# Three pairs instead of two in the token-ordered end of a seven-product down projection, four more weight buffers for it, and a new written order of all 4836 steps

## The chip, the cores and the metric

The kernel runs on one core of one Trainium2 chip. The metric is the device time of one execution in microseconds. Before the change three executions took 626.68, 627.62 and 628.64 us; the median is 627.62.

## The reference

One layer of a hybrid decoder for 512 tokens of width 1024, all in float32: a conditioned RMS norm, one input projection that feeds a gated linear recurrence (512 channels) and an eight-head sparse attention, an output projection, a residual, a second conditioned norm, and a squared-ReLU MLP with 4096 hidden features. What matters here is its end:

```python
h = modulate(rms_norm(x, pre_norm_mlp[l]), sh2, sc2)
y = jnp.square(jax.nn.relu(h @ w_ff1[l])) @ w_ff2[l]
x = x + (1.0 + g2[:, None, :]) * rms_norm(y, post_norm_mlp[l])
```

## The kernel before

**Precision.** A float32 factor is split into a high part `hi`, rounded to the format that TensorE takes at full rate, and a rest `lo` (`split_f32`: a copy on ScalarE or VectorE, then a subtraction). A product is three matmuls (`mm3`): hi by hi, hi by lo, lo by hi, each of 512 output columns here. All matmuls are recorded at line 396, transposes at 400, ScalarE work at 407, VectorE and GpSimd work at 441, loads and the stores of the output at 483.

**Down projection.** The hidden features are 32 tiles `fT[0..31]` of 128 features by 512 tokens, taken in 16 pairs (`NP`). The tokens are cut into two halves, the 1024 output columns into two halves and each pair is its own inner cut of two, so that each pair is a two-by-two block product done with seven products instead of eight. Products "6", "7" and "1" need sums of weight blocks and of token halves and are done in a first pass (`first_pass`, weights `A0` to `A15`, interleaved with the up projection). Products "2" to "5" are done in a second pass (`second_pass`, weights `B0` to `B15`). A PSUM bank tag stands for each: "2" is `f`, "3" is `s`, "4" is `pv`, "5" is `tp`, with two banks each, one for each of two 128-token blocks `t` (0 and 1) of a token half.

For each pair of the second pass two raw weight tiles, 512 KB each, are loaded; two subtractions form block differences in them; each is split into hi and lo (128 x 1024); and the two `fT` tiles of the pair are split into four `fs` tiles (`operands`). Product "2" needs the first half of the lower weight tile, "3" its second half, "4" and "5" the halves of the upper one. A pair is 4 products x 2 blocks x 3 matmuls = 24 matmuls.

**The last phase.** For the first `NP - G_LAST` = 14 pairs the loop goes pair, product, block. For the last two (`G_LAST = 2`) it goes block first: all of block 0 (4 products x 2 pairs x 3 = 24 matmuls), then all of block 1. When a product of a block is complete, VectorE and others combine it with the running sums `acc`, and `finish` computes the norm of the finished 128 output rows, scales, adds the residual and stores. `finish(t + 2, ...)` comes after product "4" of block t and `finish(t, ...)` after product "5". So while TensorE works at block 1, the other engines finish the rows of block 0. In `finish` a sum of squares runs on ScalarE (with `accum_out`), a product with `g2row` on VectorE or GpSimd (tile names `fT<-ar,g2row`), the small `stat` steps turn the sum into a scale, and a `scalar_tensor_tensor` with the residual `r` comes ahead of each store.

**Buffers.** `Weights` holds a ring of 4 raw tiles and of 4 hi/lo pairs for all weights from start to end (`RAW_BUFS`, `PART_BUFS`), `f_tile` a ring of 8 `fs` tiles, two pairs' worth. The pool `fp` holds `h2` and `h2l`, the operands of the up projection, and `g2row`.

**What sets the order.** The program is first recorded as 4836 steps, numbered in the order in which a greedy planner puts them down, and then issued in the order of the text `PLAN`: two characters are one step (90 letters, so `C^` is step 12 x 90 + 84 = 1164). Each engine's queue is that text with only the engine's own steps left in. `PLACE` gives for each step with a choice the engine: a is ScalarE, d is VectorE, p is GpSimd. Nothing is reordered at run time: an instruction that waits holds what is behind it on its engine. The steps' numbers are the same in both kernels up to the end of the up projection (step 4086), so the two texts can be compared there step by step.

**Before the MLP.** The gate branch of the recurrence (`g0` to `g3` of `proj`) leaves TensorE through one of two `f` banks; ScalarE copies each to SBUF (`act(rnn["g"][:, n, :512], ps, AF.Copy)`, recorded as `r<-f`), and the next projection in that bank waits for the copy.

Of the kernel before, what the change touches and what calls it, by code (L numbers as in the profile page):

```python
# [33 lines left out]
G_LAST = 2  # L34
# [56 lines left out]
    '000O0P020Q0106400R0S0T0U0V0M074p4q084r0a0W0y040b4sGX4t090c030&0d0X0A554u0C4v054w0e4x0(0-4y0Y0H0N4z4!0D4:'  # L91
    '4;0I0B4<0)0Z0f0E0.0,4D0J0z0/0_0=0^0K0!0{0L0|0*0g0>0h4=0?0F4>0i1O0}0j0:4?104@0~0G0]12144[0k1P0;0l0m0#110@'
    '131j1C0n0%1E0o1F0p151k1G1v171619180+1H0q1A1D540r1B1l561J1=0s1M0t1I0u1N0v1K0w1Q0x1>1U1m0$1R1T1n0[1S1W0<1L'
    '1o1V1X1w1p1q1r1]1a1s1b2M1h1x1d1t1^1@1$1Z1[201f1?1u1c1i1Y572L2X2Q2R1y1_1e1+1&2Y2S1{1g1|1!1)2N1#211}2T1-1;'
    '232&2s27221*2O1:2U1%2P1z2(292V2Z1(2x1/2v1.2t24262y2z302C1,1~2w1<2A2)2u2D2W3125282}2!322F2#2I2B2H2$2|2J2a'
    '2d372E2K2~2G3S2c2j2g2e2f382b2l2i333V3T2k39352r2h2n342/2m2q363W2*2p3X2%2o2-3*3!3U2,3x3#2<2]3c3Y2?2=3y3C3Z'
    '3I3$2:3a2{2@583d2^3O3F3D3z3b3%3e3h3&3J3n3+3P3(3L3i3o3,3R3)3t4#3k3/4H3?3u4%3:3q4F3{3@45463w3A473G3M484M2.'
    '3|3f4O494C3l3r4A3<4N4B3-4g3=4G4$4h4i4k4l4m4j4Q4^4&4n4P4+4o4,4-4]GY4(4.2+2>4~4S5L504)2;514*3]5K4/2[4_3~4{'
    '4d2_3^5Y3E413K3Q52425D3B5X5M4|4}59533H3j445E5h5A5B5C435F5H5G3N5g5J3p3v5O3g3m5I5N5S3;5$3[5P3s4b7%5T3.5R3>'
    '4a3_3}4J5Q5#5Z5U5V5a5b5i5j5k4I5-5W5l5m5d5n5o5p5q5,5r4X5s7&4V5t5u4K5e627)6;4c6-5v4L5w6<6.6/5x6=5y615z5f6d'  # L100
    '5!5%6>6e4W6f7>6N674U6_6M5c6:7(68696@6A7?6V6B6{6?6C4e4R6D5_6E5&4Z4T6g6F4Y6G6H6I6U5(5)6[6J6|7+6K4f6q6}6L7|'
    '6h6O5*6p6P6i5+6]6^816Q6~6R6j6y5.5/6S6x6T6W5:726k5{716l6X6m6n5;5<7a6Y5=5>6a5?7b5@5[6Z5]73706o7c5^5}5|6r5~'
    '6c607C636s7B646t7R6u656v6w6b667N746z6!7S7D6#6$6%8L7z757T6&7@7!766(7[7o7]7}6)7~80777*7#788279836*847A7s85'
    '7t7p6+7q86877M88897r8A8B7w7u8V8W7vGW8Z8C8D8X7x7E8b7^8K8d937F8Y947,8E7-977_7.GZ957G997H7y7I9&7/8e4E7J8j9('
    '7K8k9)7L9+7O8h8F9,7P8f6,8G8O8i9E8P8QGa987Q7U9A9F7V8R9I7W9K7X9J9G7Y8M8S7Z8g7$7d8T7:7e8c9:7fG@9H8^8_9L8{9;'
    '7g8a9<7h7i968U8|8l8}7j8~9MAO8mG]90919*929B7;8u8q8v7kAP9=AU8w9N8x7l8y8r8z8!8#9l8$G^8%8&8(8)8*8n8+G_7m9C8o'
    '8,8t8-G[9m8.9T7<8p9D8N9V7=8s8/9O8:8H8;8<8=AV8>8I9W9n8?9r9o9s9X8@9Y9Z9aAS8[9b9R9c9p9d9t9e9v9f9w9x9q9y9g9U'
    'A59z8J9h9!AQAW9#ARA67{9$9iA79%AE9SAvB.A88]7nApAF9-AGAHAq9u9.AXA9B/AwAI9/9>AT9?9@Ar9[At9]9j9^9PAAAJAgCbAB'
    'CcAY9_C9AxAK9{AD9|9}9~AZ9QCdAdAcCiA.CAA/AuA0AhAzA!CNCjCkHPA>CpCqAsA#AfA?CrA:AeA@AiC#A<A$C$A%ALC%AaAjAbAM'
    'C+A&C,COA1C-A=BDBEANC/AyBHB5C:BJC;A[BFC<A(A;AkBtBIA]A2BGACA)BKHQBLA*AlA3B6BuB1BMA+B2BRB3C=A^BPC_A_BNC>A,'  # L110
    'A|BvAmA-A~B,BwB79kBhAoC1B-HRA}B4C3C2B8HSCWBnB9BiB0CHC4HeAnA4A{CBCVCQBAHbBjBBBoCIBpB:BCBcBqBkCXCJCRBlCUBd'
    'BmCLCKBrBxCSB#CMC{BsB$ByBzCaC@B%C[C|DVC]C~B!D0CTB(D1D2DWCZD3D4D6CeD7B)ChD8CYD9DACoDBCuDCDDCmDEB*DFCsDGCf'
    'DHDICwB+DJCzDKC)DLDMClC!C^DOCvDPB;DND$CtCnD%DQDRFhD+D@C*D[DSD]CxDTDUC&DuDYDeDvDZCyDaDbDcC?BSDdDhD^D_DiDw'
    'C(DjB&DkD)BODlDyDmD!DnDzD&DoDfBeB<D{BQD|ECD,D}DpBTC}D(DqDrD*DsDxD~E6B=EDBUE0D5D#E1DtBYEsFjBZEtB?BaEuD-E2'
    'CgEvEwD.BbBfB@E7BVB[E3C.BWB]B^D=B|ExD?E*B_E+E8BXE,EAE9GUFlE4EEEaEbD/E[BgEgE]HEEhEBC5GVB}E^D;B~E_L(D<EFE{'
    'EiDXE|D>FAF%EcL&EeFBFCFnFIB{EdFJEfE-C0FKFdEjHFFeFfE5FgE=E>C6F|C7EkE?EQHJD:EGE.ElCPFkEHEmE/EWE;EIEJErC8FR'
    'FSEoEKFTEXCCFLEqELB>FoFMEYEREpCDFNEMFPENCEEOF}ESEPEZF~F&F4F5HNF,ETF-G0H>G,FiG-EUH?HKFmEyEVF6F<F=F.G3CGE}'
    'E~EzF>E!EnF0G4F1HLE#CFE$E%F2F_F7H@GxF:F8FpG.F3E&GrFUE(FqF9FrFtG6GsFuFsGvGyG/FzGtFvE)FwG:F{G1H4F!F#F$FxH5'
    'GzG;FDF(G8FyF)G2FGG9GAE@F*HGG5GBH6H[F+E:H]HAF;H^HBFHGCFOH_H8G7F@E<GDHCH{H|GEF[HpHqHOFQGNGOHHHDGPGQHrF]H7'
# [417 lines left out]
class Weights:  # L537


    def __init__(self, clk, pool, raws):  # L540
        self.clk, self.pool, self.raws, self.jobs, self.index = clk, pool, raws, [], {}
        self.queue, self.loaded, self.parts, self.raw_live, self.part_live = [], {}, {}, [], []
        self.l = self.s = 0
        self.slots, self.taken = [], {}
# [1265 lines left out]
```

## Time and profile before

| what | us |
|---|---|
| median of three executions (lowest, highest) | 627.62 (626.68, 628.64) |
| the profiled execution | 627.82 |
| its span, first to last instruction | 626.0 |
| outside the span | 1.8 |
| TensorE / VectorE / ScalarE / GpSimd busy | 596.3 / 539.2 / 346.1 / 209.1 |
| from the end of the last matmul to the end of the span | 12.0 |

The profiled execution is 0.20 us above the median. A matmul's record covers 0.39 us for 512 columns, but successive ones start 0.227 us apart, so the busy sum of TensorE says little and its waits are read from the starts. VectorE's records overlap a little as well: three successive 128 x 512 steps of 0.68 us start 0.60 us apart.

### The profile page before, as it was taken

The numbers are of one execution on the slowest core, as the hardware profiler recorded it, in microseconds if no ns is written. First come the engines' busy times: TensorE is split into PE (matmuls) and PEld (weight loads), VectorE is DVE, ScalarE is ACT, GpSimd is POOL, SyncE is SP. The second block draws the span as 40 slices with busy tenths as digits, with TensorE's granted clock in tenths as the row PEclk, the third lists the DMA queues.
The fourth block names the chain that finished last, engine by engine and source line by source line (L and its number), as shares of the span: only waits on it lengthen the run. The fifth ranks groups of instructions, "written<-read, shape, count | busy, mean of one in ns | idle before, by whom it ended". The sixth has DMA issues, their size and how long they took to land.

```text
span 626.0 us, 9043 instructions
## 1 busy us (share of the span) xinstructions
PE 596.3 (95%) x3060; PEld 497.9 (80%) x3060; DVE 539.2 (86%) x1072; ACT 346.1 (55%) x696; POOL 209.1 (33%) x209
## 2 busy tenths in 40 slices
PE   7999999998999999989999999999999999999992
PEld 6888788966777898869887888888887888878881
DVE  5986988979999988988888968787688789999897
ACT  6654525698999999687251220322322247465563
POOL 5001301652663175453204547641351231000113
PEclk9999999999999999999999999999999999999997
DMA  8968895430503302015664334254544426756613
GB/s 351 416 250 318 320 299 191 131 136 1 202 2 129 141 2 102 1 35 176 229 222 168 115 133 137 101 169 157 180 135 147 155 69 204 238 179 202 198 56 134
DMA packets 29430, 102.15 MB, mean 163 GB/s; under 512 B 3268, under 2 KB 3524, under 8 KB 29384
## 3 DMA queue, kind: packets, MB, share of 16 engines
q1 hardware_dynamic: 29240, 101.50, 46.4%
q8 instruction: 24, 0.39, 0.3%
q14 instruction: 22, 0.18, 0.1%
q10 hardware_dynamic: 144, 0.07, 0.0%
HBM read 99.47 MB, written 2.10 MB: 162 GB/s over the span
## 4 chain that ended last, share of the span: by engine, by line
PE 73%; DVE 11%; DMA 6%; ACT 5%; issue 3%; DVEq 0%; SPq 0%; ACTq 0%
PE f L396 36%; PE s L396 14%; PE pv L396 13%; PE tp L396 7%; DMA ar<-in_ada_t 4%; PE tp L400 4%; DVE r L441 3%; ACT p L407 2%; DVE fT L441 2%; ACT r L407 2%; DVE ar L441 1%; DMA raw_A11l<-in_wd 1%; DMA raw_A10l<-in_wd 1%; DVE p L441 1%; DMA r<-in_x 1%
## 5 line engine op out<-in xcount | busy, mean ns | idle before, releaser
L396 PE MATMUL f<-h,hi_f 128*128 128x512 f32 x224 | 87.7, 392 | 0.0
L396 PE MATMUL f<-h,lo_f 128*128 128x512 f32 x224 | 87.2, 389 | 0.0
L396 PE MATMUL f<-h2l,hi_f 128*128 128x512 f32 x224 | 87.2, 389 | 0.0
L407 ACT ACTIVATE fT<-f 128x512 f32<-128x512 f32 x30 | 17.8, 594 | 71.2 <-PE f L396 71.2
L396 PEld LDWEIGHTS f<-h,hi_f 128*128 128x128 f32 x224 | 42.1, 188 | 8.8 <-issue 0.2
L396 PEld LDWEIGHTS f<-h2l,hi_f 128*128 128x128 f32 x224 | 42.0, 188 | 8.6
L396 PEld LDWEIGHTS f<-h,lo_f 128*128 128x128 f32 x224 | 42.0, 188 | 8.5
L396 PE MATMUL f<-hi_o,h 128*128 128x512 f32 x128 | 47.7, 414 | 0.0
L407 ACT ACTIVATE p<-p,mx 128x32 f32<-128x32 f32 (+4 forms) x96 | 45.1, 472 | 3.8 <-DVE mx L441 3.6
L441 DVE TENSOR_TENSOR lo_f<-raw_f,hi_f 128x1024 fp32r<-128x1024 f32 x29 | 40.1, 1383 | 6.9 <-ACT hi_f L407 6.6
L400 PE MATMUL tp<-ident,p 128*128 128x128 f32 x192 | 41.6, 273 | 1.9 <-DVE pt L441 0.9
L396 PE MATMUL pv<-pt,V 128*128 128x256 f32 x160 | 42.2, 316 | 1.1 <-ACT pt L407 0.7
L441 POOL TENSOR_SCALAR p<-p,den 128x32 f32<-128x32 f32 (+4 forms) x43 | 35.7, 863 | 18.5 <-DVE den L441 15.5
L396 PE MATMUL s<-K,Q 128*128 128x288 f32 (+4 forms) x128 | 38.4, 336 | 0.5 <-DVE Q L441 0.3
L441 DVE TENSOR_TENSOR pt<-tp,pt 128x512 fp32r<-128x512 f32 (+1 forms) x56 | 33.6, 609 | 3.3 <-ACT pt L407 1.9
L407 ACT ACTIVATE hi_f<-raw_f 128x1024 fp32r<-128x1024 f32 x24 | 24.9, 1056 | 18.7 <-PE f L396 13.0
L396 PEld LDWEIGHTS pv<-pt,V 128*128 128x128 f32 x160 | 27.8, 189 | 6.1 <-DVE pt L441 2.1
L396 PE MATMUL s<-r,fs 128*128 128x512 f32 x96 | 32.5, 389 | 0.0
L396 PE MATMUL pv<-r,fs 128*128 128x512 f32 x96 | 31.8, 391 | 0.4 <-DVE r L441 0.4
L400 PEld LDWEIGHTS tp<-ident,p 128*128 128x128 f32 x192 | 25.0, 140 | 7.8 <-issue 1.8
L396 PE MATMUL tp<-r,fs 128*128 128x512 f32 x96 | 30.6, 389 | 0.0
L441 DVE CUSTOM_DVE_ANT_0 ar<-ar,silb 128x1024 f32<-128x1024 f32 x16 | 21.6, 1352 | 6.4 <-DMA ar<-in_ada_t 6.4
(732 smaller groups left out, 1817.0 us busy)
## 6 DMA issues: line engine op xcount, KB each, us to landing
raw_f<-in_wf SPq DMA_DIRECT2D x32, 512.0 KB, 3.5
p<-in_ada_a SPq DMA_DIRECT2D x16, 512.0 KB, 8.0
ar<-in_ada_t SPq DMA_DIRECT2D x16, 512.0 KB, 4.4
ar<-in_ada_r SPq DMA_DIRECT2D x16, 512.0 KB, 4.0
r<-in_x SPq DMA_DIRECT2D x8, 512.0 KB, 4.6
raw_c<-in_wc SPq DMA_DIRECT2D x8, 512.0 KB, 5.2
raw_o<-in_wo SPq DMA_DIRECT2D x8, 512.0 KB, 6.4
raw_a<-in_wa SPq DMA_DIRECT2D x8, 384.0 KB, 7.5
```

Source lines behind the costliest of these rows:

```text
L396: lambda: self.nc.tensor.matmul(out, lhs, rhs, start=start, stop=stop))
L400: self.issue("pe", 0.109, [out], [src], lambda: self.nc.tensor.transpose(out, src, ident))
L407: return "act", cost, lambda: self.nc.scalar.activation(out, src, func, scale=scale, bias=bias, **kw), func
L441: return eng, cost, lambda: fn(out, *args, **kw), None
```

## The change

`G_LAST` becomes 3: the block-first order takes in the last three pairs, 36 matmuls a block. Number and shape of all matmuls stay the same. The third pair's operands get four tiles of their own (`more`), in a buffer that the first pass used for its weights. After the up projection `fp` is closed, and a new pool `late` takes its place in SBUF, with four more raw tiles and two more hi/lo pairs; `g2row` moves to a pool of its own (`gp`) that stays. `PLAN` and `PLACE` are replaced throughout.

```diff
-G_LAST = 2
+G_LAST = 3
...
-        self.clk, self.pool, self.raws, self.jobs, self.index = clk, pool, raws, [], {}
+        self.clk, self.jobs, self.index = clk, [], {}
+        self.rings = {"raw": [(raws, RAW_BUFS)], "part": [(pool, PART_BUFS)]}
+        self.homes = {"raw": {}, "part": {}}
...
+    def room(self, what):
+
+        used = [p for homes in self.homes[what].values() for p in homes]
+        return [(p, n) for p, n in self.rings[what] for _ in range(n - used.count(p))]
+
+    def take(self, what, name):
+
+        tag = {"raw": "raw", "part": "hi"}[what]
+        ring = min(self.room(what), key=lambda r: self.clk.slot(r[0], tag, r[1]))
+        self.homes[what].setdefault(name, []).append(ring[0])
+        return ring
...
-    fp = ctx.enter_context(tc.tile_pool(name="fp", bufs=1, reuse_waits="tile"))
+    gp = ctx.enter_context(tc.tile_pool(name="gp", bufs=1, reuse_waits="tile"))
+    fp_ctx = ExitStack()
+    fp = fp_ctx.enter_context(tc.tile_pool(name="fp", bufs=1, reuse_waits="tile"))
+    g2row = [clk.lone(gp, [P, 512], F32, name=f"g2row{n}", under=(id(mp),)) for n in range(2)]
...
+    fp_ctx.close()
+    late_pool = ctx.enter_context(tc.tile_pool(name="late", bufs=1, reuse_waits="tile"))
+    clk.under[id(late_pool)] = (id(fp),)
+    W.rings["raw"].append((late_pool, 4))
+    W.rings["part"].append((late_pool, 2))
...
-        last = [nxt] + [operands(j) for j in range(NP - G_LAST + 1, NP)]
+        more = small(rp, "r8", 4, [P, 4, RW], F32R).rearrange("p a b -> p (a b)")
+        last = [nxt, operands(NP - G_LAST + 1), operands(NP - 1, [more[:, half(k)] for k in range(4)])]
```

The engines of the steps from the second pass on, one letter for each choice. First the 96 choices for the weights B0 to B15, six each (difference, difference, hi, lo, hi, lo); only these of them differ:

```
       B1       B6       B8       B15
-      ppadad   ddaddd   ddaddd   ddadad
+      ppadad   ddadad   ddadad   ddaddd
```

Then the 76 choices of `DN` (64 for the hi and lo of `fT[0..31]`, and 12 of the last phase: for each block the two sums after "2" and "3", the two products with `g2row` of `finish(t + 2)` and the two of `finish(t)`):

```diff
-    'DN': 'ddadadadadadadadadddadadapadadadadadadddadadapadadadadadadadadadddppddpppddd',
+    'DN': 'adadadadadadddadadadadadadadadadadadadadadadadadadadadadadadadadddppddddppdd',
```

Two lines of `PLAN` as they stood and two as they stand, out of 93 each. The first of each has the copy of gate tile g0 out of its bank (step 1164, `C^`) and the first matmul of g2 into that bank (step 1195, `DP`), the second the copy of g2 (step 1225, `Dt`) and the first matmul of g3 into that bank (step 1314, `Es`):

```diff
-    'DHDICwB+DJCzDKC)DLDMClC!C^DOCvDPB;DND$CtCnD%DQDRFhD+D@C*D[DSD]CxDTDUC&DuDYDeDvDZCyDaDbDcC?BSDdDhD^D_DiDw'
-    'C(DjB&DkD)BODlDyDmD!DnDzD&DoDfBeB<D{BQD|ECD,D}DpBTC}D(DqDrD*DsDxD~E6B=EDBUE0D5D#E1DtBYEsFjBZEtB?BaEuD-E2'
+    'CRBoBpBcCeBqByBzCTBrBdC{C|C~BsD0C[D1C]CZD2CoD3D4C^DVD6D7CaD8ChD9B!BOB(B#DWCYDADPB$DBCwDCDDCfDEDFCmDGDHDI'
+    'BSD)DjD!DkDeDwDlB&DmD+DnCsBTCgDoDzDpBUCyDqDxB<D|D,DrD5DsD(D}BYD~DtE0ECBVE1BaBfE2BWBZD#B@C}B[B]D*E6EsBbEt'
```

More of the change, by code (lines that the diff above doesn't have):

```diff
@@ new lines @@
+    'FA': 'pdpppdpddddd',
+    'RS': 'dpadddddadda',
+    'TH': 'dddpaadddaddaaddddddadpdddddaadd',
+    'UP': 'dddpddpdddddppdpdddpdpdddddddddd',
+    'VW': 'pddpddppdppdppppdpp',
+    'WS': 'adadadadadadadadadadadadadaddpadapapadapddaddpapadadadadaddapdadddddddddaddaddapadadpaddapdaddda'
+        'ddddddpdaddpaddaddadpapddaddaddddpadaddddapdaddapddddpaddadpddaddddaddaddadddaddaddaddadadapdadd'
+        'adpadadadddpdaddadadapdadddddadadaddddddddadadadddddaddaddaddadpadddadadppadadddadadddadadddadad'
+        'ddadadddadadddadadddadadddadadddadadddadadddadadddadadddadadddaddd',
@@ L88 @@
+    'XN': 'aaapdpaaaapa',
 }
 PLAN = (
[L91 to L95, printed above, removed]
@@ L184 @@
+    'rNrJrOrPrQq]q#rVrRrSrhrWrTriq$rjrkq!rUrlrXrmrnq{rorprZrYrqrrrsraq^rbrurcq_rfrwrdrgrxrvreryq|rzrtr!r$r#r%'
 )
@@ L562, in need @@
         return {"raw": 0, "split": 1, "b": 2}.get(kind, 0)
+    def room(self, what):
[6 more added lines that the diff above has]
+        return ring
     def action(self):
-        if self.l < len(self.queue) and len(self.raw_live) < RAW_BUFS:
+        if self.l < len(self.queue) and self.room("raw"):
             return "load"
@@ L571, in action @@
             return None
-        if len(self.part_live) + self.need(job.kind) > PART_BUFS or (job.kind in COMBOS and len(self.slots) < 2):
+        if len(self.room("part")) < self.need(job.kind) or (job.kind in COMBOS and len(self.slots) < 2):
             return None
@@ L587, in ready @@
             return t
-        return max(t, *(c.slot(self.pool, x, PART_BUFS, self.need(job.kind)) for x in ("hi", "lo")))
+        return max(t, *(min(c.slot(p, x, n) for p, n in self.rings["part"]) for x in ("hi", "lo")))
     def load(self):
         name, loads = self.queue[self.l]
-        raw = self.clk.tile(self.raws, "raw", RAW_BUFS, [P, 1024], F32, f"raw_{name}")
+        pool, bufs = self.take("raw", name)
+        raw = self.clk.tile(pool, "raw", bufs, [P, 1024], F32, f"raw_{name}")
         for view, src in loads:
@@ L596, in load @@
         self.clk.hold(raw)
-        self.raw_live.append(name)
         self.l += 1
@@ L605, in parts @@
         def parts(e=""):
-            self.part_live.append(name)
-            return [c.tile(self.pool, x, PART_BUFS, [P, 1024], F32R, f"{x}_{name}{e}")[:, :n] for x in ("hi", "lo")]
+            pool, bufs = self.take("part", name)
+            return [c.tile(pool, x, bufs, [P, 1024], F32R, f"{x}_{name}{e}")[:, :n] for x in ("hi", "lo")]
         if job.kind == "raw":
@@ L637, in split @@
         for r in job.free:
-            self.raw_live.remove(r)
+            del self.homes["raw"][r]
             c.live.discard(self.loaded[r].tensor.name)
@@ L665, in drop @@
         if job.kind == "raw":
-            self.raw_live.remove(name)
+            del self.homes["raw"][name]
             self.clk.live.discard(self.loaded[name].tensor.name)
@@ L670, in drop @@
         else:
-            for _ in range(self.need(job.kind)):
-                self.part_live.remove(name)
+            del self.homes["part"][name]
 def split_f32(c, hi, lo, src):
@@ L1521, in block_kernel @@
     mp_ctx.close()
-    fp = ctx.enter_context(tc.tile_pool(name="fp", bufs=1, reuse_waits="tile"))
+    gp = ctx.enter_context(tc.tile_pool(name="gp", bufs=1, reuse_waits="tile"))
+    fp_ctx = ExitStack()
+    fp = fp_ctx.enter_context(tc.tile_pool(name="fp", bufs=1, reuse_waits="tile"))
+    g2row = [clk.lone(gp, [P, 512], F32, name=f"g2row{n}", under=(id(mp),)) for n in range(2)]
     h2 = [clk.lone(fp, [P, 512], F32R, name=f"h2_{k}", under=(id(mp),)) for k in range(KD)]
     h2l = [clk.lone(fp, [P, 512], F32R, name=f"h2l_{k}", under=(id(mp),)) for k in range(KD)]
-    g2row = [clk.lone(fp, [P, 512], F32, name=f"g2row{n}", under=(id(mp),)) for n in range(2)]
     ffs = {}
@@ L1666, in between, with split_f, operands @@
             dve("tensor_add", acc[0, t], acc[0, t], bk["7"][t])
-    def split_f(f):
-        fh, fl = f_tile(), f_tile()
+    def split_f(f, room):
+        fh, fl = (room.pop() if room else f_tile() for _ in range(2))
         split_f32(clk, fh, fl, fT[f])
         return fh, fl
-    def operands(j):
-        (lh, ll), (uh, ul) = split_f(2 * j), split_f(2 * j + 1)
+    def operands(j, room=()):
+        (lh, ll), (uh, ul) = split_f(2 * j, room), split_f(2 * j + 1, room)
         return {"2": (lh[:, U], ll[:, U]), "3": (lh[:, L], ll[:, L]), "4": (uh[:, U], ul[:, U]),
```

202 lines of the change are left out of this document (98 added, 104 removed).

## Prediction

> **What bounds the kernel now.** I read the page first, for the busy shares and the chain that ended last.
>
> ```profile
> span 626.0 us, 9043 instructions
> PE 596.3 (95%) x3060; PEld 497.9 (80%) x3060; DVE 539.2 (86%) x1072; ACT 346.1 (55%) x696; POOL 209.1 (33%) x209
> PE 73%; DVE 11%; DMA 6%; ACT 5%; issue 3%; DVEq 0%; SPq 0%; ACTq 0%
> ```
>
> TensorE carries 73% of the chain, VectorE (DVE) 11%. The matmuls stay the same, so only waits and the end can move. Then the busy times by stretch: 100 to 205 is attention and gates, 510 to 526 the end of the first pass, 526 to 604 the second pass, from 604 on the last phase and what follows the last matmul.
>
> ```profile
> core 0: us, PE busy (x) PEld busy (x) DVE busy (x) ACT busy (x) POOL busy (x), PEclk, DMA share, GB/s
> 100.00:205.00 105.00, 98.75 (x546) 79.51 (x547) 96.71 (x296) 93.68 (x245) 50.24 (x49) 1.00 0.31 111
> ...
> 510.00:526.00 16.00, 16.00 (x71) 12.95 (x69) 15.15 (x29) 9.57 (x16) 0.00 (x0) 1.00 0.37 124
> 526.00:604.00 78.00, 77.47 (x341) 63.66 (x340) 73.46 (x93) 44.74 (x58) 6.90 (x4) 1.00 0.58 191
> 604.00:614.00 10.00, 10.00 (x45) 8.00 (x43) 9.28 (x18) 5.44 (x15) 4.62 (x4) 1.00 0.00 0
> 614.00:623.20 9.20, 0.04 (x1) 0.00 (x0) 9.15 (x20) 3.19 (x10) 2.79 (x2) 0.72 0.44 171
> 623.20:626.00 2.80, 0.00 (x0) 0.00 (x0) 0.00 (x0) 0.00 (x0) 0.00 (x0) 0.50 0.48 187
> ```
>
> See that TensorE has almost no idle time from 510 to 614 (0.53 us), that it has 6.25 us in 100 to 205, where VectorE and ScalarE are nearly full too, and that VectorE is busy for 9.15 of the 9.20 us after the last matmul. So the end is a VectorE queue, then 2.8 us of stores. VectorE is nearly the bound before that as well: from 510 to 604 it idles 0.85 + 4.54 = 5.4 us.
>
> The timeline of the last phase and of the end, and the rows of the stores:
>
> ```profile
> 602.14 1.23 DVE L441 TENSOR_TENSOR lo_B15b<-raw_B15l,hi_B15b 128x1024 fp32r<-128x1024 f32 x1 [0.43 <-ACT hi_B15b L407]
> 602.93 0.39 PE L396 MATMUL f<-hi_B14b,fs 128*128 128x512 f32 x1
> 604.49 1.22 DVE L441 TENSOR_TENSOR lo_B15b<-raw_B15u,hi_B15b 128x1024 fp32r<-128x1024 f32 x1
> 606.85 0.39 PE L396 MATMUL pv<-hi_B15b,fs 128*128 128x512 f32 x1
> 607.27 0.69 DVE L441 TENSOR_TENSOR fT<-fT,pv 128x512 f32<-128x512 f32 x1
> ...
> 613.51 1.55 POOL L441 TENSOR_TENSOR ar<-ar,fT 128x512 f32<-128x512 f32 x1 [1.24 <-ACT fT L407]
> 613.65 0.39 PE L396 MATMUL tp<-hi_B15b,fs 128*128 128x512 f32 x1
> ...
> 615.05 0.68 DVE L441 TENSOR_TENSOR fT<-fT,g2row 128x512 f32<-128x512 f32 x1
> 615.14 1.73 POOL L441 TENSOR_TENSOR fT<-ar,g2row 128x512 f32<-128x512 f32 x1
> 615.65 0.68 DVE L441 TENSOR_TENSOR fT<-fT,tp 128x512 f32<-128x512 f32 x1
> 616.25 0.68 DVE L441 TENSOR_TENSOR ar<-ar,tp 128x512 f32<-128x512 f32 x1
> 617.36 0.63 ACT L407 ACTIVATE junk<-ar 128x512 bf16<-128x512 f32 x1
> 617.58 0.14 DVE L441 TENSOR_SCALAR stat<-stat 128x1 f32<-128x1 f32 x1
> 617.99 0.19 ACT L407 ACTIVATE stat<-stat 128x1 f32<-128x1 f32 x1
> 618.30 0.15 DVE L441 RECIPROCAL stat<-stat 128x1 f32<-128x1 f32 x1
> 621.74 1.41 DVE L441 SCALAR_TENSOR_TENSOR fT<-fT,stat,r 128x512 f32<-128x512 f32 x2
> DMA to landing us min/median/max: 2.0/2.0/2.1
> ```
>
> The last product is ready at about 614.07 (the row at 607.27 starts 0.42 us after its last matmul), but VectorE comes to it only at 615.65: it is still at block 0's and product "4"'s work. The last store's data is there at 623.15.
>
> **The change part by part.** The 4836 steps and their matmuls, loads and stores are the same in number. What moves is order, engine and buffers.
>
> *Three pairs block-first: the end.* The last phase starts with the row at 602.93 and has 48 matmuls, 47 gaps to 613.65, or 0.228 us each. With 72 it starts 24 x 0.228 = 5.47 us earlier, at 597.46, and ends at the same 613.65 if TensorE isn't starved. Block 0 is then complete 12 x 0.228 = 2.7 us earlier, and block 1's first products lie further ahead of its end, so VectorE's queue should be empty but for the last when the last matmul ends. What is then left for VectorE after 614.07: two sums with `tp` and two products with `g2row`, 4 x 0.60; four `scalar_tensor_tensor`, 2 x 1.41; eight small `stat` steps at 0.07 to 0.15, about 0.8. That is 2.4 + 2.8 + 0.8 = 6.0 us, to 620.1, and the stores add 2.8: 622.9, 3.1 us before 626.0. That is one end, with half of this work (`finish(3)`) wholly after 614.07. The other end is the bare chain of the last product: two sums (1.28), its square with the readout, about 0.9, the `stat` steps through sqrt (0.14, 0.19, 0.15 and handovers, about 1.0), two last steps 1.41: 614.07 + 4.6 = 618.7, stores to 621.5, a gain of 4.5. Two sums for block 1 move from GpSimd (1.55 for one at 613.51) to VectorE (0.68), which shortens the way to `finish(3)`, and one of its products moves to GpSimd. I take 3.3, near the first end, since the windows show VectorE back to back.
>
> *What this asks of VectorE before.* B15's lower lo is read by the eighth matmul of the phase: now at 597.46 + 7 x 0.228 = 599.06. Before, its step ended at 603.37. The upper one is read by the eighth matmul of product "4": 597.46 + 25 x 0.228 = 603.2, and was ready at 605.71. So all weight splits must be done 2.5 us earlier, and those of B15's lower half 4.3 us; the latter partly by going ahead of B14's upper half. The cover is VectorE's idle time of 5.4 us from 510 on. The engine list adds to it: one hi copy less (-0.6), two copies of fs less (-0.7), two fs rests more from GpSimd (+1.2), two sums more (+1.2), one product less (-0.6), so +0.5 by the 0.60 us pitch. That fits: 2.5 + 0.5 of 5.4. If it is not covered, TensorE waits at about 599 for up to 4.3 us.
>
> *Second pool and own operand tiles.* Four more raw tiles and two more hi/lo pairs let loads and splits run one pair further ahead. The pool lies where h2 and h2l were, so its first load waits for the last matmul of the up projection, near 513.6; loads queued behind it on SP wait too, but SP has only loads there, in the order of need. That wait costs nothing as long as B0 still lands before the second pass at 526, and with the DMA engines 0.37 busy in 510 to 526 there is room. The gain is at most TensorE's 0.53 us idle in 526 to 604. I take 0; the buffers are what makes the 2.5 us possible.
>
> Those 0.53 us have their cause in two rows:
>
> ```profile
> 551.16 1.36 POOL L441 TENSOR_TENSOR fs<-fT,fs 128x512 fp32r<-128x512 f32 x1 [21.59 <-ACT fs L407]
> 551.27 2.32 DVE L441 TENSOR_TENSOR lo_B5b<-raw_B5u,hi_B5b 128x1024 fp32r<-128x1024 f32 x1
> 554.25 0.74 PE L396 MATMUL f<-hi_B5b,fs 128*128 128x512 f32 x2 [0.53 <-DVE fs L441]
> ```
>
> A VectorE step of 1.22 (the row at 604.49) took 2.32 beside a GpSimd product. The new list has no GpSimd step there, but four of the eight late `g2row` products (before: three). [...]
>
> *The new order before the MLP.* TensorE's waits in 100 to 205, and what ScalarE did before the first:
>
> ```profile
> PE f L396 <- ACT r L407: 2.9, 2, 1.9
> 140.53 2.57 ACT L407 ACTIVATE r<-r,sp 128x512 f32<-128x512 f32 x4
> 144.41 1.15 ACT L407 ACTIVATE r<-r 128x512 f32<-128x512 f32 x2
> 146.94 0.60 ACT L407 ACTIVATE r<-f 128x512 f32<-128x512 f32 x1
> 147.59 0.50 PE L396 MATMUL f<-h,hi_g 128*128 128x512 f32 x1 [1.91 <-ACT r L407]
> ```
>
> The gate copy at 146.94 stood behind four exponentials, two roots and more. In the old text no TensorE step lies between that copy and the first of g2 (`C^DOCvDP`), nor between the next copy and g3 (`DtBYEs`). In the new text eight lie between in both places, and the first copy is ahead of the roots. So both waits, 2.9 us, can go. But the work of ScalarE and VectorE (96.71 and 93.68 of 105) is not less, and what is put behind the copies is late next: exponentials, roots, the attention's copies. Ends: -2.9, and +2.9 if as much turns up elsewhere. I take half of the gain, -1.4. Elsewhere the order is new too; I found no place with a sign and take 0.
>
> **Sum.** 627.82 - 3.3 - 1.4 = 623.1 on the profiled execution's scale; that is 0.20 above the median of the runs, so 622.9.
>
> **The rivals.**
>
> 1. *TensorE is starved at the start of the last phase* and the clock falls (the other side). A bunch of waits at 274 to 280 shows the price:
>
> ```profile
> 276.00:280.00 4.00, 2.25 (x15) 1.81 (x15) 3.89 (x7) 3.47 (x7) 2.19 (x2) 1.00 0.23 70
> 280.00:284.00 4.00, 4.00 (x21) 4.00 (x22) 3.33 (x5) 3.38 (x5) 0.55 (x1) 0.57 0.25 77
> ```
>
> After 1.75 us idle in four the granted clock was 0.57 for four, which costs 4 x 0.43 = 1.7. A full stall of 4.3 and this are 6.0 against the 3.3: 627.6 + 6.0 - 3.3 = 630.3; with the early gain it would be 628.9, no change. It decides when stall and clock cost over 5.2 (3.3 and the 1.9 of resolution), or over 6.6 with the early gain. For it: VectorE is at 94% there. Against: 5.4 idle for 3.0. [...]
>
> 2. *Partly starved:* a stall of 2 to 4 without the clock, which gives back the tail: 622.9 + 3.3 = 626.2, no change. For it: lo steps wait for ScalarE's hi (0.43 at 602.14), so not all idle time is usable.
>
> 3. *GpSimd's late products hold VectorE up,* by 1.3 (their row at 551 is 1.36): 624.2. [...]
>
> 4. *Early order all gain, bare chain at the end:* 627.62 - 4.5 - 2.9 = 620.2.
>
> 5. *The early waits come back elsewhere* (+2.9): 627.62 - 3.3 + 2.9 = 627.2, no change.
>
> **Chances and range.** Forecast (622 to 624) 0.42; rival 4 and what lies towards it (below 622) 0.23; rival 3 or a small stall (624 to 625.7) 0.14; rivals 2 and 5 (within 0.3% of 627.62, that is 625.7 to 629.5, about what a measurement can tell from no change) 0.14; rival 1 (above) 0.07. So faster 0.79, same 0.14, slower 0.07. The range goes from rival 4 to just past rival 2: 620.0 to 626.6, which leaves out some 0.07 below and 0.12 above.
>
> **What would show it.** Right: the last matmul at about 612 with no wait near 599; VectorE reaches the last product within 0.3 us of its end; last matmul to end of span about 8.7 us instead of 12.0; no wait of TensorE for `ACT r` over 0.5 us. Wrong: a TensorE wait for `lo_B15b` or `hi_B15b`; VectorE windows after the last matmul still 9 us full; TensorE's idle time in 100 to 205 still over 6 us; a clock below 1 in a stretch where it was 1.00.

## The result, and the profile after

The changed kernel took 624.22 us (median of 20 runs, 620.63 to 628.45) against 627.70 us for the kernel before in the same session: ratio 0.9937, 95% interval 0.9917 to 0.9957. A second session gave 623.37 against 629.06, ratio 0.9909 (0.9876 to 0.9941). By these two ratios the kernel is 0.6 and 0.9% faster. The profiled execution is the fastest of its 20 runs (620.63 us, span 618.9), so the difference of 7.1 us between the two profiles is about twice that of the medians. For this reason I read single stretches from several profiles below.

The page of the changed kernel: span, busy times, engines of the chain that ended last.

```profile
span 618.9 us, 9038 instructions
PE 592.5 (96%) x3060; PEld 495.3 (80%) x3060; DVE 529.2 (86%) x1061; ACT 349.3 (56%) x713; POOL 199.4 (32%) x203
PE 87%; DVE 7%; ACT 2%; DMA 1%; issue 1%; POOL 0%; DVEq 0%; ACTq 0%
```

TensorE's share of the chain went from 73% to 87%, VectorE's from 11% to 7%. Busy times by stretch (columns as in the prediction; the last phase begins at 592.15 and the last matmul ends at 608.64):

```profile
100.00:205.00 105.00, 98.28 (x545) 79.82 (x544) 96.84 (x287) 96.05 (x254) 58.16 (x55) 1.00 0.31 112
510.00:526.00 16.00, 15.34 (x67) 12.04 (x66) 14.12 (x22) 10.85 (x17) 4.62 (x3) 1.00 0.82 295
526.00:597.00 71.00, 70.97 (x314) 58.44 (x313) 69.33 (x90) 43.12 (x57) 0.00 (x0) 1.00 0.49 164
597.00:608.30 11.30, 11.30 (x52) 9.30 (x50) 9.82 (x21) 6.25 (x18) 4.75 (x4) 1.00 0.06 24
608.30:616.10 7.80, 0.34 (x2) 0.00 (x0) 7.58 (x16) 1.68 (x6) 0.84 (x1) 0.67 0.43 167
```

TensorE is full from 526 to the last matmul. The 0.53 us stall near 553 is gone and no weight split of the last phase is late. After the last matmul VectorE is again full until the last stores (7.58 of 7.80). In 510 to 526 TensorE now idles 0.66 us, which it did not before. TensorE's only wait from 500 on (us in total, times, longest):

```profile
PE f L396 <- DVE lo_B0b L441: 0.6, 1, 0.6
```

The timeline around the last matmul, and VectorE's last step:

```profile
607.86 1.28 POOL L441 TENSOR_TENSOR fT<-fT,g2row 128x512 f32<-128x512 f32 x1
607.86 1.83 DVE L441 SCALAR_TENSOR_TENSOR fT<-fT,stat,r 128x512 f32<-128x512 f32 x1
608.25 0.39 PE L396 MATMUL tp<-hi_B15b,r 128*128 128x512 f32 x1
609.68 0.67 DVE L441 TENSOR_TENSOR fT<-fT,tp 128x512 f32<-128x512 f32 x1
...
614.58 1.41 DVE L441 SCALAR_TENSOR_TENSOR fT<-fT,stat,r 128x512 f32<-128x512 f32 x2
```

The last product can be taken 0.42 us after its matmul starts, at 608.67. VectorE takes it at 609.68, 1.0 late: a scaled sum that elsewhere lasts 0.75 us took 1.83 beside a product on GpSimd. From the end of the last matmul to the end of the span are 10.2 us, where there were 12.0.

### The profile page after: what moved, and what is told of

The parts are those of the page before. It is cut to its first block, busy times and chain, and to the rows that moved or that the text cites. A ratio compares the mean times of both kernels' runs of the same rounds, so it can differ in the third digit from the quotient of the medians.

```text
span 618.9 us, 9038 instructions
## 1 busy us (share of the span) xinstructions
PE 592.5 (96%) x3060; PEld 495.3 (80%) x3060; DVE 529.2 (86%) x1061; ACT 349.3 (56%) x713; POOL 199.4 (32%) x203
## 4 chain that ended last, share of the span: by engine, by line
PE 87%; DVE 7%; ACT 2%; DMA 1%; issue 1%; POOL 0%; DVEq 0%; ACTq 0%
PE f L396 44%; PE s L396 17%; PE pv L396 13%; PE tp L396 8%; PE tp L400 4%; DVE fT L441 2%; DVE r L441 1%; ACT h L407 1%; DVE p L441 1%; DMA raw_B0l<-in_wd 1%; DVE pt L441 1%; DMA vecs<-in_vecs 1%; ACT junk L407 1%; POOL p L441 0%; DVE ar L441 0%
## 5 line engine op out<-in xcount | busy, mean ns | idle before, releaser
L441 POOL TENSOR_SCALAR p<-p,den 128x32 f32<-128x32 f32 (+4 forms) x42 | 42.6, 1024 | 16.8 <-DVE den L441 9.8
L400 PE MATMUL tp<-ident,p 128*128 128x128 f32 x192 | 43.9, 275 | 3.2 <-DVE pt L441 2.5
L396 PE MATMUL s<-K,Q 128*128 128x256 f32 (+4 forms) x128 | 38.8, 340 | 2.8 <-DVE mx L441 2.1
L441 DVE TENSOR_TENSOR lo_f<-raw_f,hi_f 128x1024 fp32r<-128x1024 f32 x29 | 36.8, 1275 | 3.5 <-ACT hi_f L407 3.3
L396 PE MATMUL tp<-r,fs 128*128 128x512 f32 x96 | 32.0, 389 | 0.0
L441 POOL TENSOR_TENSOR fs<-ft,fs 128x256 fp32r<-128x256 f32 x14 | 17.9, 1278 | 40.5 <-ACT fs L407 27.3
L441 DVE SCALAR_TENSOR_TENSOR accT<-ar,sil,accT 128x512 f32<-128x512 f32 x32 | 26.3, 823 | 3.8 <-DMA ar<-in_ada_r 3.7
```

Source lines behind the costliest of these rows:

```text
L396: lambda: self.nc.tensor.matmul(out, lhs, rhs, start=start, stop=stop))
L400: self.issue("pe", 0.109, [out], [src], lambda: self.nc.tensor.transpose(out, src, ident))
L441: return eng, cost, lambda: fn(out, *args, **kw), None
```

## Where the time went, run by run

All times are medians. "Up" is the start of the up projection, "tail" the time from the end of the last matmul to the end of the span, "B0" TensorE's wait for `lo_B0b`; these three are from the profiled execution, in us. The ratio is to the kernel before in the same session.

| run | time | ratio (95%) | up | B0 | tail |
|---|---|---|---|---|---|
| before | 627.7 to 629.1 | 1 | 276.1 | 0 | 12.0 |
| after | 624.2 | 0.9937 (0.9917 to 0.9957) | 272.2 | 0.6 | 10.2 |
| e1_after_again | 623.4 | 0.9909 (0.9876 to 0.9941) | 273.1 | 0.6 | 10.2 |
| e2_old_early | 625.0 | 0.9928 (0.9900 to 0.9957) | 277.6 | 1.4 | 10.2 |
| e3_new_early | 627.9 | 0.9970 (0.9945 to 0.9994) | 274.9 | 0.2 | 12.0 |
| e4_tail_vector | 623.6 | 0.9908 (0.9875 to 0.9941) | 274.3 | 1.7 | 10.2 |
| e5_two_pairs | 628.6 | 0.9992 (0.9969 to 1.0015) | 274.4 | 1.7 | 13.7 |
| e6_no_raw_pool | 666.3 | 1.0586 (1.0545 to 1.0627) | 273.5 | 0 | 10.2 |
| e7_b0_in_new_pool | 624.3 | 0.9918 (0.9891 to 0.9946) | 276.3 | 1.9 | 10.2 |
| e8_early_to_115us | 624.0 | 0.9926 (0.9900 to 0.9953) | 277.0 | 1.7 | 10.2 |
| e9_tail_less_work | 622.6 | 0.9910 (0.9881 to 0.9940) | 275.8 | 1.7 | 9.2 |
| e10_b0_pool_lower_first | 622.2 | 0.9901 (0.9874 to 0.9928) | 274.6 | 0 | 10.2 |
| e12_three_pairs_alone | 631.8 | 1.0045 (1.0019 to 1.0071) | 274.1 | 0.3 | 10.2 |
| e13_best | 622.4 | 0.9899 (0.9869 to 0.9929) | 275.6 | 0 | 9.7 |

## Experiments: which part gains

The list of steps was cut at step 2428, just before the up projection, and the halves of the two lists were joined.

```
e1  the changed kernel once more
e2  PLAN, PLACE: before's first 2428 steps, then after's; three pairs, second pool
e3  PLAN, PLACE: after's first 2428 steps, then before's; two pairs, one pool
```

> The changed kernel once more, as a second profile and for the times. If its first profile (620.63 us) is typical, this one has the up projection at 272 us, the last matmul's end at 608.6 and 10.3 us after it. If the median of its 20 runs (624.22) is, the profile is 2 to 5 us longer; the theory that the excess lies before the MLP then has the up projection at 274 to 277 and the stretch from the last matmul to the end at 10.3 again; the rival that the end varies has the up projection at 272 and more than 12 after the last matmul.

> The old written order and engines for the first 2428 steps (up to the first matmul of the up projection), the new ones from there on, with three pairs and the second pool. Theory, the gain is shared: 625 to 626.5 us, that is the 1.7 us at the end and what the up projection gives, and the up projection begins at 276 as before. Rival, it is all in the order before the MLP: 627 to 628. Rival, it is all behind it: 624 to 624.5.

> The counterpart: the new written order and engines for the first 2428 steps, from there on the old order, two pairs, no second pool. Theory, shared: 625.5 to 627 us, the up projection at 272 to 275, 12 us after the last matmul as before. Rival, all in the order before the MLP: 624 to 624.5. Rival, all behind it: 627.5 to 628.

The profile of e1 is close to the first one (273.1 and 10.2 us), and its execution too took less than the median (621.5 against 623.4 us), so where the longer ones lose time stays open. In the session of e1 to e3 the kernel before took 629.06 us, 1.4 more than in the first one, so I go by the ratios here and not by the times that were expected. The late part alone gives 0.7% (e2), the early order alone 0.3% (e3); multiplied they are 0.9898, beside the 0.9937 and 0.9909 of the whole. Most of the gain seems to stand behind the start of the MLP, though the intervals of e2 and e3 overlap a little.

One piece of it I had not seen. From the first matmul of the up projection to the start of its last group of three the kernels with the old late order take 236.7 (before), 235.8 (e3) and 235.7 us (e12, below), and all with the new one 234.9 to 235.2. The granted clock (the column after POOL's) shows where. Busy times by stretch in after, whose up projection starts at 272.2:

```profile
272.00:276.00 4.00, 2.85 (x20) 2.52 (x21) 3.97 (x8) 3.95 (x8) 0.88 (x3) 1.00 0.30 85
276.00:280.00 4.00, 3.12 (x24) 2.71 (x23) 3.90 (x5) 3.10 (x5) 0.00 (x0) 1.00 0.29 86
280.00:284.00 4.00, 4.00 (x36) 4.00 (x35) 3.51 (x5) 3.27 (x6) 1.43 (x3) 1.00 0.72 234
```

and in e12, three pairs in the old order, which starts it at 274.1:

```profile
274.00:278.00 4.00, 2.49 (x15) 1.96 (x15) 3.90 (x7) 3.47 (x8) 2.19 (x2) 0.90 0.24 54
278.00:282.00 4.00, 4.00 (x24) 4.00 (x25) 3.33 (x5) 3.39 (x5) 0.55 (x1) 0.67 0.26 97
```

In the new order TensorE's idle time is spread (1.15 us, then 0.88) and the clock column stays at 1.00; in the old order it idles 1.51 us in one stretch and the next has 0.67 and 24 matmuls in place of 36. That the spreading is what keeps the clock up is not shown: further on, e12 waits once for 2.6 us without a drop and once for 2.0 us with one (next section). The prediction quotes the same drop (0.57) as the price in a rival, and does not ask whether the new order keeps it.

## Experiments: three pairs and the second pool

```diff
 e5: after, with
-G_LAST = 3
+G_LAST = 2
 e6: after, without
-    W.rings["raw"].append((late_pool, 4))
 e12: before's PLAN and PLACE with G_LAST = 3 and the last phase of after,
-    W.rings["raw"].append((late_pool, 4))
+    loads and splits of B10 to B15 moved 1 to 5 us ahead
```

> The kernel after with the last phase over two pairs again; the second pool, the new order (the steps of the moved pair put back among the earlier ones, everything else in place) and the new engines stay. If the third pair is what shortens the end: last matmul to end of the span 12.0 us instead of the 10.2 to 10.3 of the three runs that have three pairs, time 1.7 above the kernel after (about 626.0). If the new late order alone shortens it: 10.2 us and a time within 0.5 of the kernel after. In both cases the start of the up projection stays near 273 and the clock between 265 and 300 stays at 1.00.

> The kernel after with three pairs and the two extra pairs of split tiles, but without the four extra tiles for unsplit weights: B0 to B2 then load one after another into the four old tiles. If the second pool is worth nothing (the prediction's price of 0): time within 0.6 of the kernel after, TensorE's wait for lo_B0b as it is (0.6 to 1.7), and at most 0.5 of waiting for lo_B1b and lo_B2b. If the early loads of B1 and B2 pay: waits for these two of over 1 us, matmuls of the first pairs of the second pass late, a time 1 to 3 us above the kernel after. If the extra loads only stand in the way of B0 on the queue: the wait for lo_B0b falls below 0.3 and the time is 0.5 to 1 us lower.

> The kernel before (its early order, its late order, its engines, four unsplit tiles) with three pairs in the last phase and two more pairs of split tiles, but without the four extra unsplit tiles: steps and engines of the last phase from the kernel after, loads and splits of B10 to B15 moved ahead by 1 to 5 us, everything else as before. If the third pair is what gains: last matmul to end 10.2 us instead of 12.0, no TensorE wait of over 0.3 in the second pass, start of the up projection at 276 as before, time 1.5 to 2 us below the kernel before. If three pairs need the second pool: TensorE waits for lo_B14b or lo_B15b of over 1 us near the start of the last phase, which eat the gain, time within 0.5 of before or above it.

The third pair without the pool (e12) does shorten the tail to 10.2, but TensorE waits 4.6 us: 2.6 until 592.50, ahead of the last phase, and 2.0 until 601.47, in it. The time is 0.45% above before. TensorE's waits of e12, and the busy times by stretch behind each of them:

```profile
PE f L391 <- DVE fs L436: 2.6, 1, 2.6
PE f L391 <- DVE lo_B15b L436: 2.0, 1, 2.0
...
594.00:598.00 4.00, 4.00 (x19) 3.31 (x18) 3.69 (x6) 3.62 (x6) 0.00 (x0) 1.00 0.14 56
601.50:605.00 3.50, 3.50 (x9) 2.79 (x10) 2.25 (x3) 0.00 (x0) 0.00 (x0) 0.51 0.00 0
```

Behind the second wait the granted clock is 0.51 for 3.5 us, by my estimate 3.5 x 0.49 = 1.7 us more. Waits and clock together are 6.3 us. That is the prediction's rival 1, about at its place and at its size (6.0); at the ratio 1.0045 the first session's 627.7 would be 630.5, and rival 1 without the early gain was 630.3.

The timeline of e12 on VectorE and on the queue:

```profile
588.63 1.23 DVE L436 TENSOR_TENSOR lo_B13b<-raw_B13l,hi_B13b 128x1024 fp32r<-128x1024 f32 x1 [0.67 <-ACT hi_B13b L402]
600.20 1.22 DVE L436 TENSOR_TENSOR lo_B15b<-raw_B15l,hi_B15b 128x1024 fp32r<-128x1024 f32 x1
...
589.88 0.33 SPq L478 DMA_DIRECT2D raw_B15l<-in_wd  x1
```

The first load of B15 goes out at 589.88, 28 us before the last matmul's end (618.1). VectorE waits five times for ScalarE's hi halves from 560 to 602, 2.6 us in all, and so cannot use all of its 3.35 us of idle time there. The timeline of after:

```profile
575.57 0.33 SPq L483 DMA_DIRECT2D raw_B15l<-in_wd  x1
...
591.66 1.22 DVE L441 TENSOR_TENSOR lo_B15b<-raw_B15l,hi_B15b 128x1024 fp32r<-128x1024 f32 x1
595.74 1.22 DVE L441 TENSOR_TENSOR lo_B15b<-raw_B15u,hi_B15b 128x1024 fp32r<-128x1024 f32 x1
```

With eight unsplit tiles the load of B15 goes out 33 us before the end of the last matmul, and VectorE splits it as soon as its turn comes. The hand-made order of e12 is not a searched one, so e12 shows that the old order moved ahead does not do; it does not show that no order could. The kernel after without the four tiles (e6; 543 of the 4836 places of its `PLAN` differ from after's) takes 38 us more than before, where 1 to 3 more than after were expected: VectorE's steps stand in a row made for loads that go ahead, and now each waits for a load that waits for the split before it. VectorE's largest waits of e6:

```profile
DVE raw_B9u L436 <- DMA raw_B9l<-in_wd: 5.2, 1, 5.2
DVE raw_B7u L436 <- DMA raw_B7u<-in_wd: 4.0, 1, 4.0
```

and its busy times over the second pass:

```profile
526.00:604.00 78.00, 61.89 (x223) 46.89 (x221) 45.87 (x60) 31.34 (x41) 0.00 (x0) 0.87 0.41 135
```

TensorE is busy for 61.89 of 78 us at a clock of 0.87 there. With pool and order but two pairs (e5) the gain is gone as well: the tail is 13.7 us and TensorE waits 1.0 for an operand split near 599. Neither of my two theories for e5 foresaw that; the order was made for a longer last phase, and I take that for the reason, without having shown it. So the third pair without pool and late order (e12), pool and order without the third pair (e5), and pair and order without the pool (e6) all show no gain. The pool alone and the late order alone were not run.

## Experiments: the new wait for B0

After, and every variant of it that loads B0 to B2 as it does, waits 0.6 to 1.7 us for `lo_B0b` as the second pass begins; the prediction gave that place 0. My first theory was a late load: in after, B0's tiles wait until A14 is split, their loads go out 3.3 and 4.5 us after the last group of three matmuls of the up projection begins (507.4), and VectorE idles 1.18 us for one.

```diff
 e7: B0 and B1 lie in the second pool, B2 in the old tiles
+        if name in ("B0l", "B0u", "B1l", "B1u"):
+            ring = self.rings["raw"][1]
-    queue: B2u B0u B0l B1l B1u B3u B2l B3l
+    queue: B1u B0l B0u B1l B2l B2u B3l B3u
 e10: e7, and VectorE and ScalarE take B0's lower half first
-    raw_B0u, raw_B0l; hi, lo of B0u; hi, lo of B0l
+    raw_B0l, raw_B0u; hi, lo of B0l; hi, lo of B0u
```

> The kernel after, but the two unsplit tiles of B0 and those of B1 lie in the second pool, and those of B2 in the old tiles that the last up-projection weights (A14) leave; the queue issues B1u, B0l, B0u, B1l and then B2. If B0 is late because its tiles wait for A14's splits (issues at 510.7 and 511.9, VectorE idle 1.2 us for it at 515.8): B0 is issued by 509, that idle is gone, TensorE's wait for lo_B0b falls from 0.6 (up to 1.7 in the other runs) to below 0.2, first up-projection weight group to first matmul of the second pass shrinks from 12.8 to about 12.3, time 0.5 to 0.8 below the kernel after. If VectorE's own queue of A15 splits sets it: the wait stays within 0.3 of what it is and the time within 0.3.

> The run with B0 in the second pool (its issue early, VectorE's idle 1.2 us gone, and yet a wait of 1.9 us for lo_B0b), with the lower half of B0, which the first products read, subtracted and split ahead of the upper half, as against the upper half first. Theory: the wait came from VectorE's two lo_B0b splits of 2.32 and 2.30 us beside GpSimd's subtractions of B1 (1.22 us each when alone), with the half that is needed first done second: with the halves exchanged the first split ends some 2.3 us earlier, TensorE's wait for lo_B0b is at most 0.2, last up-projection group to the first matmul of the second pass 12.3 to 12.6 us, and last phase and end 1.5 to 2 us earlier against that start than in the run before: time 622.3 to 623.5 on the scale of the kernel after at 624.2. Rival: TensorE waits for the operand fs or for the upper half instead: the wait only moves, the time stays within 0.4 of the run before.

In e7 the first load of B0 goes out 1.3 us after that group begins, VectorE's idle time is gone, and yet the wait is 1.9 us. So the early load alone does not cure it. The timeline of VectorE and GpSimd in e7:

```profile
521.55 2.32 DVE L436 TENSOR_TENSOR lo_B0b<-raw_B0u,hi_B0b 128x1024 fp32r<-128x1024 f32 x1
523.80 2.30 DVE L436 TENSOR_TENSOR lo_B0b<-raw_B0l,hi_B0b 128x1024 fp32r<-128x1024 f32 x1
...
519.83 2.96 POOL L436 TENSOR_TENSOR raw_B1l<-raw_B1l,raw_B1u 128x512 f32<-128x512 f32 x1 [4.54 <-DMA raw_B1l<-in_wd]
522.75 2.27 POOL L436 TENSOR_TENSOR raw_B1u<-raw_B1u,raw_B1l 128x512 f32<-128x512 f32 x1
```

and in after:

```profile
518.77 1.23 DVE L441 TENSOR_TENSOR lo_B0b<-raw_B0u,hi_B0b 128x1024 fp32r<-128x1024 f32 x1
519.91 1.22 DVE L441 TENSOR_TENSOR lo_B0b<-raw_B0l,hi_B0b 128x1024 fp32r<-128x1024 f32 x1
521.04 1.78 DVE L441 TENSOR_TENSOR fs<-fT,fs 128x512 fp32r<-128x512 f32 x1
...
520.43 1.85 POOL L441 TENSOR_TENSOR raw_B1l<-raw_B1l,raw_B1u 128x512 f32<-128x512 f32 x1 [9.20 <-PE s L396]
```

GpSimd subtracts B1's halves, in both kernels (B1's letters in `PLACE` are the same). Before, B1 came so late that this ran behind B0's splits:

```profile
524.73 1.22 DVE L441 TENSOR_TENSOR lo_B0b<-raw_B0l,hi_B0b 128x1024 fp32r<-128x1024 f32 x1
527.02 1.29 POOL L441 TENSOR_TENSOR raw_B1l<-raw_B1l,raw_B1u 128x512 f32<-128x512 f32 x1 [17.12 <-DMA raw_B1l<-in_wd]
```

The second pool brings B1 earlier, and the two engines meet. In e7 each of VectorE's splits takes 2.3 us in place of 1.22. In after VectorE's second split had begun first: it keeps its 1.22, GpSimd's step takes 1.85 in place of 1.29, and only VectorE's next step is lengthened (at 521.04, 1.78 where such a step takes 0.68 elsewhere). In e2, e4, e5, e8 and e9 the second of the two splits is hit (2.30 to 2.32) and the wait is 1.4 to 1.7; in after and e1 neither is, and it is 0.6.

For these 0.6 us the late load fits. In after B0's second load lands after 4.9 us, with B1's two loads sent 0.4 and 0.9 us behind it; in e6, which sends B1 only 3 us later, the same load, sent as long after that group, lands after 4.0 us, VectorE idles 0.25 in place of 1.18, and TensorE does not wait for `lo_B0b`:

```profile
516.95 0.69 DVE L441 TENSOR_TENSOR raw_B0u<-raw_B0u,raw_B0l 128x512 f32<-128x512 f32 x1 [1.18 <-DMA raw_B0l<-in_wd]
...
517.29 0.69 DVE L436 TENSOR_TENSOR raw_B0u<-raw_B0u,raw_B0l 128x512 f32<-128x512 f32 x1 [0.25 <-DMA raw_B0l<-in_wd]
```

The first row is of after, the second of e6. In e7 VectorE begins its splits 2.35 us ahead of the first matmul of the second pass, where after has 1.39; at 1.22 us each they would have been in time, by my estimate. So e7 mended this part, and the meeting with GpSimd cost more than it gained.

The half that the first products read is the second to be split. In e10, which is e7 but for that order, both steps still take 2.32 and 2.31 us, but the needed half comes first: the wait for `lo_B0b` is gone, and all that is left from 500 to the last matmul in TensorE's waits is

```profile
PE pv L391 <- DVE ar L436: 0.5, 1, 0.5
```

The median is 622.2 against e7's 624.3 (other session), ratio 0.9901 against 0.9918: in the expected direction, with intervals that overlap. The trace settles the wait, the medians alone would not.

## Experiments: the tail

```diff
 e4: DN's choices 72 and 73, the last two products on GpSimd
-pp
+dd
 e9: these two take 8 of 512 columns
-            either("tensor_mul", o[n], a, g2row[n])
+            w = slice(0, 8) if t == 3 else slice(0, 512)
+            either("tensor_mul", o[n][:, w], a[:, w], g2row[n][:, w])
 e13: e10, with DN's choices 72 and 73
-pp
+pd
```

> The changed kernel with the two products with g2row of finish(3) on VectorE instead of GpSimd; nothing else moves. Theory, a GpSimd product holds VectorE up (a step of 0.75 took 1.83 beside one): no such step over 0.8 us after the last matmul, 1.1 us won and 1.2 us of work added on VectorE, so the stretch from the last matmul to the end stays within 0.3 of 10.3 and the time the same. Rival, the products hide on GpSimd and cost VectorE nothing: 1.2 us longer, 11.5.

> The kernel after, but the two row products of the fourth block (on GpSimd at the end) take 8 of their 512 columns, so that block's output lacks the factor elsewhere; nothing else changes. Theory: VectorE's work sets the end, and part of the missing 1.5 us of the tail went to the step beside GpSimd's product (1.83 instead of 0.75 us): that step is back at 0.75, VectorE reaches the last product within 0.3 us of its matmul instead of 1.0, last matmul to end of the span 9.1 to 9.3 us instead of 10.2. Rival: the chain from the last sum through ScalarE's squares and statistics to the last store sets the end: 10.0 to 10.3 us as it is.

> The run with B0 in the second pool and its lower half first, and in the tail one of GpSimd's two row products (the second, which began beside VectorE's 1.83 us step) on VectorE; the other stays on GpSimd. If VectorE's work sets the end: the step is back at 0.75, one product of 0.6 us is added to VectorE, last matmul to end 9.6 to 9.8 us instead of 10.2, no wait for lo_B0b, time 0.3 to 0.6 below the run with both on GpSimd (622.2), which is at the edge of what five rounds tell; ratio to before 0.988 to 0.991. If the end hangs on the chain through the statistics: 10.2 us and the same time.

With both products on VectorE (e4) the slow step is gone, two products of 0.6 us are added, and the tail stays 10.2. With nearly no work in them (e9) it is 9.2. The timeline of e9's end has the step back at 0.75 and VectorE at the last product in time (last matmul 613.02, taken at 613.45):

```profile
612.62 0.75 DVE L441 SCALAR_TENSOR_TENSOR fT<-fT,stat,r 128x512 f32<-128x512 f32 x1
613.02 0.39 PE L396 MATMUL tp<-hi_B15b,r 128*128 128x512 f32 x1
613.45 0.69 DVE L441 TENSOR_TENSOR fT<-fT,tp 128x512 f32<-128x512 f32 x1
```

With one product moved (e13) it is 9.7. So VectorE's work, counted step by step, sets the end, and the chain through ScalarE's statistics does not. The best versions that compute everything are e10 (622.2 us) and e13 (622.4 us, ratio 0.9899, 0.9869 to 0.9929). In time they are not told apart from each other (the 0.3 to 0.6 us that e13 was to gain did not show), nor, with any certainty, from after.

## Experiment: where the early gain lies

```
e8  PLAN, PLACE: after's first 885 steps (to about 115 us), then before's up to step 2428, then after's
```

> The changed order and engines for the first 885 steps (to about 115 us) and again from the up projection on; between them the old order and engines, with the old waits for the two copies of the gates (2.9 us). If the early gain lies in the stretch 45 to 100 us, as the lost TensorE time there (5.8 before, 1.6 to 2.4 with the new order) says: TensorE busy about 39.9 of 40 us in 60 to 100, first up-projection matmul at 272 to 274.5, time within 0.6 of the kernel after though the wait for the gate copies is back. If it lies in these gate waits, as the prediction had it: first up-projection matmul at 276 to 277.6, time 1.5 to 2.5 above the kernel after, close to the run with the whole early order old.

The two signs disagree: its time is that of the kernels with the whole new order (e7, same session, 624.3), but its up projection starts at 277.0, as in the old one. The wait for the gate copies is back, as built (`PE f` for `ACT r`, 3.0 us). TensorE is busy for 38.55 of the 40 us from 60 to 100, not 39.9; 1.4 us of that stretch are a wait for the load of `raw_c`. The start of the up projection turned out to be a poor judge: it lies at 274.1 to 277.6 in three profiles with the old early order and at 272.2 to 276.3 in ten with the new (means 275.9 and 274.5). One cause of the spread is that wait for `raw_c`: 0.6 in e1, 1.2 in e5, which has the same early order, and 2.4 in e2. Another is which execution was profiled: that of e8 took 2.0 us more than its median, that of after 3.6 less. From 45 to 100 us TensorE idles 3.1 us before and 3.5 in e2, and 0.0 to 1.2 in the ten, but in e12, with the old early order, only 1.3. Where the early order gains stays open.

## Why the prediction was right, and which of its steps were not

The forecast was 622.9 in a range of 620.0 to 626.6, and the time is 624.2. Step by step:

- **No starvation of the last phase: right, but its cover was reckoned too simply.** VectorE had B15's upper half split at 596.96. The prediction let 5.4 us of idle VectorE time cover the earlier splits and named the buffers only as what makes it possible. In e12, without the pool's unsplit tiles and in the old order moved ahead by hand, the same earlier splits cost TensorE 4.6 us and then the clock, while VectorE idled from 560 to 602 for 0.7 us behind a load and 2.6 us behind ScalarE's hi. That the pool is what turns such idle time into usable time fits e12 and e6, but neither takes away the pool alone.
- **The tail, -3.3: mis-sized, it is -1.8.** The matmuls went as described, but the queue was not empty when the last product came: it was taken 1.0 late rather than within 0.3, and VectorE was still full behind the last matmul. About 1.0 of the missing 1.5 is the pair of products on GpSimd (10.2 to 9.2 in e9), through one slowed VectorE step. That is rival 3, which the prediction priced at 1.3 and put at a small chance (at 615 before GpSimd's step had grown to 1.73, and VectorE's had kept its 0.68); the time of 624.2 lies in its band, not in that of the forecast (622 to 624). The rest is in the main VectorE's work after the last product: 6.3 us (609.68 to 615.99) where 6.0 were counted, with five scaled sums in place of four.
- **Second pass free of waits: wrong at its start.** `lo_B0b` cost 0.6 to 1.7. The prediction asked when B0 lands and found room on the DMA engines (0.37 busy in 510 to 526, but 0.82 after). It did not ask what B1's earlier loads do to B0's, nor what B1, landing earlier, sets going on GpSimd.
- **The early order, -1.4: wrong in mechanism, and near in size by luck.** The wait for the gate copies is gone, as said, but TensorE's idle time in 100 to 205 did not fall (6.25 before, 6.72 after; over 6 was one of the prediction's own signs of being wrong). It waits elsewhere, and for the same amounts in e1, e3 and e5. TensorE's two largest waits in that stretch, after:

```profile
PE tp L400 <- DVE pt L441: 2.5, 3, 1.2
PE s L396 <- DVE mx L441: 2.1, 2, 1.9
```

  That is rival 5, where ScalarE and VectorE at over 90% were the argument. What the early order still gives, 0.3% in e3 (an interval from 0.06 to 0.55%), lies somewhere else.
- **Left out: the clock at 280** (0.57 before and 1.00 after in 280 to 284), worth 0.5 to 1.6 us by my estimate: 0.5 from the up projection's 235.7 us in e12 against at most 235.2 in the new order, 1.6 from before against e1.

From the profile of before to that of e1, whose waits I can name: start of the up projection -2.9 (-1.4 by the means above), the up projection -1.6, its last group to the second pass +0.6, second pass and last phase -0.6, tail -1.8. With the mean for the first, -4.8; with a `lo_B0b` wait of 1.7, as most runs have it, -3.7. The medians of the two sessions differ by 3.5 and 5.7. So the forecast came out near in part by luck: its tail was 1.5 too large, its early term rests on a wait that came back elsewhere, and a gain (the clock) and a cost (`lo_B0b`) that it lacked partly cancel.

## What to carry to other kernels

Ask of an earlier load not only whether it lands in time but which engine it sets going, and beside what: here the second pool brought B1 ahead and put GpSimd's subtraction beside the split that TensorE waits for (2.3 us in place of 1.22 in e7, and a wait of 1.9). Split first the half that is read first; in e10 both splits still took 2.3 us, and TensorE's wait for `lo_B0b` was gone. VectorE's idle time was no cover in e12, where it stood behind ScalarE's hi for 2.6 us while TensorE lost 4.6, nor in e6, where it stood behind a load for up to 5.2 us at a time, so list the load and the partner's step behind each idle stretch before counting it.

## What the hardware showed that I had not expected

Where the two engines meet at B0 in e7, VectorE and GpSimd mostly take turns, and a step takes 1.0 to 1.1 us more (2.32 and 2.30 in place of 1.22 on VectorE, 2.27 in place of 1.29 on GpSimd), a little less than the other's step takes elsewhere. In the rows of e7 above GpSimd's subtraction of B1's lower half ends at 522.79; VectorE's first split, begun at 521.55, ends at 523.87, 1.08 later; GpSimd's second, begun at 522.75, ends at 525.02, 1.15 after that; VectorE's second split ends at 526.10, 1.08 after that. The turns are not strict: GpSimd's first step, begun at 519.83, had let three VectorE steps in a row go ahead (begun at 519.75, 520.35 and 520.95, 0.68 each), and what decides this the rows do not show. So two steps of VectorE in a row paid for GpSimd twice, 2.2 us in all, though GpSimd had only two steps to do. In four other meetings the two begin within about a tenth of a microsecond of each other. In the timeline of after, 1.75 us ahead of the step of 1.83, GpSimd is the one that is lengthened:

```profile
606.01 0.73 DVE L441 SCALAR_TENSOR_TENSOR fT<-fT,stat,r 128x512 f32<-128x512 f32 x1
606.11 1.80 POOL L441 TENSOR_TENSOR fT<-ar,g2row 128x512 f32<-128x512 f32 x1 [4.43 <-DVE stat L441]
606.66 0.68 DVE L441 TENSOR_TENSOR fT<-fT,pv 128x512 f32<-128x512 f32 x1
```

GpSimd begins 0.10 after VectorE and takes 1.80 in place of 1.28. At 607.86 both begin together and VectorE's 0.75 becomes 1.83, GpSimd's 1.28 stays. At 615 before, VectorE had begun 0.09 ahead: it kept its 0.68, and GpSimd's step grew to 1.73. At 551 before, GpSimd had begun 0.11 ahead: it took 1.36, and VectorE 2.32 in place of 1.22. So in the three of these four where one step began first, that one kept its length or nearly, though GpSimd's first step in e7, which began 0.08 behind one VectorE step and ahead of two more, took 2.96. The prediction reckoned with the longer step of 551 for where the engines were seen to meet, and not for where an earlier load would make them meet.
